# Keeping the residual stream in the output and adding the down parts there by accumulating transfers, with four instead of three of eight gate and up quads by seven products

## The chip, the cores and the metric

The kernel runs on one core of a Trainium2 chip. The metric is the device time of one execution in microseconds (us), as a median of runs. TensorE (PE) multiplies, VectorE (DVE) and ScalarE (ACT) work on what stands in the on-chip memories, GpSimd (POOL) does a little arithmetic and issues a few transfers, SyncE (SP) issues nearly all transfers. Weights come from HBM. They are too large to stay on the chip, so each is read once, while the multiplications run.

## The reference

One layer on an input of 256 rows and 2048 columns, all in float32. The first half mixes tokens with two attentions and two gates and ends in the projection `w_o`, which is added to the input. The second half, which the change touches, is this:

```python
    x = x + (g[:, :, 0] * y_a + g[:, :, 1] * y_b) @ w_o

    gt, up = jnp.split(rms_norm(x, g_ffn) @ w_gate_up, 2, axis=-1)
    return x + (jax.nn.silu(gt) * up) @ w_down
```

`w_gate_up` is 2048 by 2 x 5632, `w_down` is 5632 by 2048.

## The kernel before, in words

**Precision.** Every float32 operand is split into a high and a low part (`h`, `l`) of the type fp32r, and one product of matrices is three matmuls with 512 columns: high by high, high by low, low by high (`mm3`, L427, L428, L429). The high part is a cast on ACT (L220), the low part a subtraction on DVE (L221 for weights, `wl`; it needs the cast).

**Stages.** First the input projection, the attentions, the gates and `w_o` in groups of 512 output columns (PSUM tile `g`). Then the feed-forward half: the 11 column blocks of 512 of the hidden layer are cut into five `PARTS`, one of three blocks and four of two. A part runs its gate and up groups, one per block, and then adds its share of the down projection, in four groups of 512 output columns.

**Quads.** A gate and up group has eight quads, q0 to q7. A quad takes 256 rows of `w_gate_up` and both halves, gate and up: two blocks of rows (256 tokens are two tiles of 128) by two blocks of columns, each with two steps of 128 rows, which is eight products or 24 matmuls. Quads in `FAST`, here q2, q4 and q6, form the same by Winograd's form of Strassen's method with seven products, 21 matmuls. It needs sums of the weight blocks (L844 to L847: four additions of 128x512 on DVE), a split of the raw blocks besides (`rh`, `rl` of 128x1024 and `r` of 128x512), and seven sums of the activations, made once per quad by `job_h` (`hs`, `hsh`, `hsl`). The split of the sums (`wh`, `wl`, 128x2048) is what a plain quad also has. `split_fast` of a fast quad is called before `split` of the quad ahead of it.

**PSUM.** The gate and up groups use all eight banks, held in four tiles: `mA` (products 1 and 6), `mB` (7, 5), `sC` (3, 2), `sD` (4, 0). Fast quads write all but bank 0, plain quads only `sC` and `sD`. After the last fast quad `evac_fast` takes `mA` and `mB` (L663 to L667), after q7 `evac_pair` takes `sC` and `sD` (L677 to L680), applies silu and the product, and a job transposes the result for the down projection. The next group's q0 can write `sC` and `sD` only after that.

**Residual.** `x1[0]` to `x1[3]`, 128x1024 each, hold the residual stream in SBUF from `evac_wo` to the end. Each part's `evac_down` adds a PSUM tile into one of them on DVE (L703), the last part stores the sum.

**Order and buffers.** Up to the last two `w_o` groups the program's order is the code's. From there a list scheduler orders each engine's queue by its own estimates, so the same code can come out in another order. Weight tiles `x` (one quad or four down steps, 1 MB as two transfers of 512 KB) have 3 buffers, so the load of one waits for the `wl` of the third before it. `wh` and `wl` share 6 buffers of 8 KB, enough for three quads, so the cast of a quad waits until PE is done with the third before it. Everything else, `x1`, `rh`, `rl`, `r`, the activations' splits, the group results, comes from 28 buffers of 4 KB (`t4`).

Of the kernel before, what the change touches and what calls it, by code (L numbers as in the profile page):

```python
# [15 lines left out]
ALU = mybir.AluOpType  # L16
# [3 lines left out]
P = 128  # L20
S = 256
NT = S // P
# [17 lines left out]
PARTS = ((0, 3), (3, 5), (5, 7), (7, 9), (9, 11))  # L40
PRIO = 200
NPAIR = KD // 2
FAST = (2, 4, 6)


class Job:
    def __init__(self, gen, after=()):
        self.gen, self.after, self.ready, self.done = gen, tuple(after), 0, False
# [25 lines left out]
class Quad:  # L74


    def __init__(self, group, i):
        self.group, self.i, self.fast = group, i, i in FAST
        plain = [k for k in range(NPAIR) if k not in FAST]
        self.first, self.last = i == plain[0], i == plain[-1]  # L80
        self.first_fast, self.last_fast = i == FAST[0], i == FAST[-1]

# [13 lines left out]
def layer_kernel(ctx: ExitStack, tc: tile.TileContext, a: dict, out: bass.AP):  # L96
    nc = tc.nc
# [11 lines left out]
    def t4(shape, name, dt=F32):  # L109
        return tp.tile(shape, dt, name=name, tag="t4")  # L110

    def small(shape, name):
        return cp.tile(shape, F32, name=name)
# [30 lines left out]
    od = out[0].rearrange("(t p) d -> p t d", p=P)  # L144
# [44 lines left out]
    def gain(name, k):  # L189
        if name == "g_mix":  # L190
            return gmix[:, k:k + 1]
        i = gat[name] + k
        return gcol[:, i:i + 1]

    def rstd_of(ss, d, name):
        n = math.prod(ss.shape[1:])
        v = small(list(ss.shape), name + "_v")
        r = small(list(ss.shape), name)
        nc.gpsimd.tensor_scalar(v, ss, 1.0 / d, EPS, op0=ALU.mult, op1=ALU.add)
        flat = (lambda z: z) if len(ss.shape) == 2 else (lambda z: z.rearrange("p a b -> p (a b)"))  # L200
        nc.gpsimd.tensor_tensor(flat(r), flat(v), mhalf[:, :n], op=ALU.pow)
        return r
# [401 lines left out]
    x1, hP, hjobs, xres = {}, {}, {}, {}  # L604
    ss2 = small([P, NT, 4], "ss2")

    def load_xres(j):
        xres[j] = t4([P, NT, 512], f"xres{j}")
        nc.sync.dma_start(xres[j], xd[:, :, j * 512:(j + 1) * 512])
# [3 lines left out]
    def job_h(i):  # L613

        ps = half_side(f"tr_h{i}").rearrange("p (k s) -> p k s", s=S)
        for k in range(2):
            f = 2 * i + k
            for t in range(NT):
                nc.tensor.transpose(ps[:, k, t * P:(t + 1) * P], x1[f // 4][:, t, (f % 4) * P:(f % 4 + 1) * P], ident)
        g = [gain("g_ffn", 2 * i + k) for k in range(2)]  # L620
        if i not in FAST:
            hP[i] = t4([P, 2, 2, S], f"hP{i}", F32R)
            split_evac(*((hP[i][:, 0, k], hP[i][:, 1, k], ps[:, k], g[k]) for k in range(2)))
        else:
            v, l, h = t4([P, 8, P], f"hs{i}"), t4([P, 7, P], f"hsl{i}", F32R), t4([P, 7, P], f"hsh{i}", F32R)
            nc.scalar.activation(v[:, 0:8:7], ps[:, 0].rearrange("p (t s) -> p t s", t=NT), AF.Copy, scale=g[0])
            nc.scalar.activation(v[:, 1:3], ps[:, 1].rearrange("p (t s) -> p t s", t=NT), AF.Copy, scale=g[1])
            nc.vector.tensor_sub(v[:, 3], v[:, 7], v[:, 2])
            nc.vector.tensor_sub(v[:, 4], v[:, 7], v[:, 0])
            nc.vector.tensor_sub(v[:, 5], v[:, 0], v[:, 3])  # L630
            nc.vector.tensor_sub(v[:, 6], v[:, 1], v[:, 5])
            split_pair(h, l, v[:, :7])
            hq[i] = (h, l)
        return
        yield

    def evac_wo(j):
        def evac(ps, step):
            x1[j] = t4([P, NT, 512], f"x1_{j}")
            nc.vector.tensor_add(x1[j], ps, xres[j])  # L640
            sq = t4([P, NT, 512], f"sq1_{j}")
            for t in range(NT):
                nc.scalar.activation(sq[:, t], x1[j][:, t], AF.Square, accum_out=ss2[:, t, j:j + 1])

            for i in (2 * j, 2 * j + 1):
                hjobs[i] = Job(job_h(i))
                hjobs[i].ready = step + 2
                jobs.append(hjobs[i])
            if j == 3:
                s = small([P, NT], "ss2s")  # L650
                nc.vector.tensor_reduce(s, ss2, axis=AX.X, op=ALU.add)
                st["2"] = rstd_of(s, DM, "r2")
        return evac
# [16 lines left out]
    def evac_pair(half, i, last):  # L670

        def evac(zu, step):
            q = held["q"]
            z, u = zu
            add, sub = nc.vector.tensor_add, nc.vector.tensor_sub
            with tc.high_priority(offset=PRIO):
                add(z[:, 1], q[0], z[:, 1])  # L677
                add(z[:, 0], q[3], z[:, 0])
                add(u[:, 0], q[2], u[:, 0])  # L679
                sub(u[:, 1], q[4], u[:, 1])  # L680
            r = st["2"]
            for t in range(NT):
                nc.scalar.activation(z[:, t], z[:, t], AF.Silu, scale=r[:, t:t + 1])
            for t in range(NT):
                nc.vector.scalar_tensor_tensor(z[:, t], u[:, t], r[:, t:t + 1], z[:, t], op0=ALU.mult, op1=ALU.mult)

            def job():
                ps = held["D" if last else "A"].rearrange("p t (k s) -> p (t k) s", s=S)
                for k in range(4):
                    for t in range(NT):  # L690
                        nc.tensor.transpose(ps[:, k, t * P:(t + 1) * P], z[:, t, k * P:(k + 1) * P], ident)
                h, l = hidT[half].tiles(i)
                split_evac((h, l, ps, None))
                return
                yield
            djobs[half, i] = Job(job())
            djobs[half, i].ready = step + 2
            jobs.append(djobs[half, i])
        return evac

    def evac_down(half, j):
        def evac(ps, step):
            nc.vector.tensor_add(x1[j], ps, x1[j])  # L703
            if half == len(PARTS) - 1:
                nc.sync.dma_start(od[:, :, j * 512:(j + 1) * 512], x1[j])
        return evac

    def evac_last(ps, t):
        for c in range(t + 1):
            w = 512 // (t + 1)  # L710
            s = slice(w * c, w * (c + 1))
            nc.vector.tensor_add(x1[3][:, t, s], ps[:, s], x1[3][:, t, s])
            (nc.scalar if c else nc.sync).dma_start(od[:, t, 1536 + w * c:1536 + w * (c + 1)], x1[3][:, t, s])
# [41 lines left out]
    for half, (j0, j1) in enumerate(PARTS):  # L755
        js = range(j0, j1)
        hidT[half] = Act(f"hid{half}", 4 * len(js))
        for i, j in enumerate(js):
            needs = {k: (lambda k=k: [hjobs[k]]) for k in range(NPAIR)}
            needs[FAST[0]] = lambda: list(hjobs.values())  # L760
            if i:
                needs[FAST[0]] = lambda half=half, i=i: [djobs[half, i - 1]]
            groups.append(Group(W["w_gate_up"], 512 * j, 1024, range(NPAIR), None, evac_pair(half, i, i == len(js) - 1), needs))
        for j in range(4):
            wd = W["w_down"][js[0] * 512:(js[-1] + 1) * 512]
            groups.append(Group(wd, 512 * j, 512, range(4 * len(js)), hidT[half], evac_down(half, j),
                                {k: (lambda k=k, half=half: [djobs[half, k // 4]]) for k in range(4 * len(js))}))
# [161 lines left out]
    def gidx(fn_name, nth=0):  # L929
        return [i for i, n in enumerate(names) if f".{fn_name}." in n][nth]  # L930

    def at(gi, fn, ahead=8):
        early.setdefault(max(0, first_step[gi] - ahead), []).append(fn)
# [9 lines left out]
    for j in range(4):  # L943
        at(gidx("evac_g0", j), lambda j=j: load_bias(j))
        at(gidx("evac_g1", j), lambda j=j: load_bias(4 + j))
        at(gidx("evac_wo", j), lambda j=j: load_xres(j))

    after_evac = {}
    after_evac[gidx("evac_b", 0)] = lambda: jobs.append(prep["kr"])
    after_evac[gidx("evac_b", 6)] = lambda: limited.extend(attn["dil", p] for p in range(4))  # L950
# [28 lines left out]
    for i, (c, ks, first, last) in enumerate(steps):  # L979
# [18 lines left out]
        ps = products(i)  # L998
# [61 lines left out]
```

## Time and profile before

| | |
|---|---|
| median of 3 runs | 1356.28 us (1355.2 to 1356.44) |
| the profiled execution | 1356.11 us, span 1354.3 us |
| around the span | 1.8 us |
| PE busy | 1339.5 us (99%) |
| PE weight loads | 1126.0 us (83%) |
| DVE busy | 949.1 us (70%) |
| ACT busy | 652.2 us (48%) |
| POOL busy | 34.3 us (3%) |
| from HBM, to HBM | 253.97 MB, 2.10 MB |

Durations overlap: matmuls are pipelined, so an engine's pace is read from the starts of neighbouring instructions, not from how long one is shown. A group row gives the count, the busy time, the mean of one in ns, and after the second bar the idle time of the engine just before these, with what ended it. The feed-forward half begins at about 634 us; each part's stretch is its gate and up groups and then the down chunks.

### The profile page before, as it was taken

To read this page: it belongs to the slowest core of one execution; us is meant where nothing else is said; L and a number is where in the kernel's file an instruction comes from. 1 tells how busy PE (TensorE), PEld (TensorE's weight loads), DVE (VectorE), ACT (ScalarE), POOL (GpSimd) and SP (SyncE) were. 2 spreads that over 40 slices of the span, in tenths; PEclk is the share of its full clock that TensorE was granted. 3 is DMA by queue.
4 is the path that set the end of the run, shared out by engine and by line. 5 is a ranking of instruction groups with operands and counts; after the bars stand their busy time and mean duration, and the time that the engine had idled before them with its cause. 6 is when DMAs were issued, how large, how long until landed. Compare 5 with 4: busy or idle time off the path is not lost.

```text
span 1354.3 us, 16169 instructions
## 1 busy us (share of the span) xinstructions
PE 1339.5 (99%) x6243; PEld 1126.0 (83%) x6243; DVE 949.1 (70%) x949; ACT 652.2 (48%) x724; POOL 34.3 (3%) x41
## 2 busy tenths in 40 slices
PE   8999999999999999999999999999999999999998
PEld 6899999988888888888788888888878888888886
DVE  5566777677645655567789756886798579857973
ACT  6455555454444444455455434454445345534541
POOL 1011112000000000000000000000000000000000
PEclk9999999999999999999999999999999999999999
DMA  7555555656556766676546665565457654754662
GB/s 247 179 175 161 161 170 167 184 161 176 174 186 205 212 188 202 209 235 207 201 158 213 221 187 183 191 213 190 157 185 245 191 186 172 229 190 163 214 214 93
DMA packets 138205, 257.14 MB, mean 190 GB/s; under 512 B 9192, under 2 KB 28688, under 8 KB 138128
## 3 DMA queue, kind: packets, MB, share of 16 engines
q1 hardware_dynamic: 137760, 255.96, 58.9%
q8 instruction: 49, 0.80, 0.2%
q14 instruction: 28, 0.23, 0.1%
q10 hardware_dynamic: 144, 0.13, 0.0%
q0 software_dynamic: 224, 0.01, 0.0%
HBM read 253.97 MB, written 2.10 MB: 189 GB/s over the span
## 4 chain that ended last, share of the span: by engine, by line
PE 94%; DVE 2%; issue 1%; DMA 1%; ACT 1%; SPq 0%; DVEq 0%; ACTq 0%
PE g L429 14%; PE g L427 14%; PE g L428 13%; PE sC L427 6%; PE sC L429 6%; PE sC L428 6%; PE mA L427 4%; PE mA L429 4%; PE mA L428 4%; PE sD L429 4%; PE sD L427 4%; PE sD L428 4%; PE mB L428 3%; PE mB L429 3%; PE mB L427 3%
## 5 line engine op out<-in xcount | busy, mean ns | idle before, releaser
L220 ACT CAST wh<-x 128x1024 fp32r<-128x1024 f32 (+3 forms) x349 | 465.3, 1352 | 437.0 <-DVE x L847 127.7
L221 DVE TENSOR_TENSOR wl<-x,wh 128x2048 fp32r<-128x2048 f32 x132 | 300.8, 2289 | 134.5 <-ACT wh L220 132.7
L221 DVE TENSOR_TENSOR wh<-x,wh 128x1024 fp32r<-128x1024 f32 (+2 forms) x217 | 250.6, 1172 | 113.1 <-ACT wh L220 111.9
L427 PE MATMUL g<-wh,xTh 128*128 128x512 f32 (+1 forms) x544 | 210.6, 387 | 0.6 <-ACT xTh L212 0.6
L429 PE MATMUL g<-wh,xTl 128*128 128x512 f32 (+1 forms) x544 | 207.9, 382 | 0.6 <-DVE xTl L217 0.6
L428 PE MATMUL g<-wh,xTh 128*128 128x512 f32 (+1 forms) x544 | 207.9, 382 | 0.0
L429 PEld LDWEIGHTS g<-wh,xTl 128*128 128x128 f32 x544 | 102.8, 189 | 17.6 <-DVE xTl L217 1.4
L427 PEld LDWEIGHTS g<-wh,xTh 128*128 128x128 f32 x544 | 102.8, 189 | 15.9 <-ACT xTh L212 0.9
L428 PEld LDWEIGHTS g<-wh,xTh 128*128 128x128 f32 x544 | 102.9, 189 | 15.4 <-DVE wh L221 0.4
L427 PE MATMUL sC<-wh,hP 128*128 128x512 f32 x220 | 86.1, 391 | 1.6 <-DVE u L679 1.5
L429 PE MATMUL sC<-wh,hP 128*128 128x512 f32 x220 | 85.7, 390 | 0.0
L429 PE MATMUL sD<-wh,hP 128*128 128x512 f32 x220 | 85.7, 389 | 0.0
L428 PE MATMUL sC<-wl,hP 128*128 128x512 f32 x220 | 85.7, 389 | 0.0
L427 PE MATMUL sD<-wh,hP 128*128 128x512 f32 x220 | 85.7, 389 | 0.0
L428 PE MATMUL sD<-wl,hP 128*128 128x512 f32 x220 | 85.7, 389 | 0.0
L220 ACT CAST rh<-x 128x1024 fp32r<-128x1024 f32 x33 | 34.7, 1051 | 36.1 <-DMA x<-in_w_gate_up_dram 36.1
L427 PEld LDWEIGHTS sC<-wh,hP 128*128 128x128 f32 x220 | 41.3, 188 | 12.3 <-issue 4.0
L427 PE MATMUL g<-wh,mTh 128*128 128x512 f32 x128 | 50.5, 394 | 0.0
L429 PE MATMUL g<-wh,mTl 128*128 128x512 f32 x128 | 49.9, 390 | 0.0
L428 PE MATMUL g<-wh,mTh 128*128 128x512 f32 x128 | 49.9, 390 | 0.0
L427 PEld LDWEIGHTS sD<-wh,hP 128*128 128x128 f32 x220 | 41.3, 188 | 8.6
L428 PEld LDWEIGHTS sD<-wl,hP 128*128 128x128 f32 x220 | 41.3, 188 | 8.6
(675 smaller groups left out, 2390.7 us busy)
## 6 DMA issues: line engine op xcount, KB each, us to landing
x<-in_w_gate_up_dram SPq DMA_DIRECT2D x176, 512.0 KB, 4.7
x<-in_w_down_dram SPq DMA_DIRECT2D x88, 512.0 KB, 5.0
x<-in_w_in_dram SPq DMA_DIRECT2D x79, 512.0 KB, 4.2
x<-in_w_in_dram SPq DMA_DIRECT2D x56, 448.0 KB, 3.6
x<-in_w_o_dram SPq DMA_DIRECT2D x32, 512.0 KB, 4.4
x<-in_w_o_mla_dram SPq DMA_DIRECT2D x16, 512.0 KB, 4.9
x<-in_w_o_dil_dram SPq DMA_DIRECT2D x16, 512.0 KB, 4.6
x<-in_w_ukv_dram SPq DMA_DIRECT2D x8, 512.0 KB, 4.0
```

Of the source, the lines that this page charges most:

```text
L220: nc.scalar.copy(h, x)
L221: nc.vector.tensor_sub(l, x, f32(h))
L427: nc.tensor.matmul(ps, ah, bh, start=first, stop=False)
L428: nc.tensor.matmul(ps, ah, bl, start=False, stop=False)
L429: nc.tensor.matmul(ps, al, bh, start=False, stop=last)
```

## The change

`FAST` gets q5 as a fourth quad, next to q4 and q6. The residual stream no longer stays in SBUF. After `w_o`, each `x1[j]` is stored to the output. A down part but the last is copied from PSUM to SBUF on ACT (`y`) and added to the output by a transfer that accumulates in memory, issued from POOL. Ahead of the last part's down groups the four tiles are loaded back on the SP queue (`load_x1`), and the end is as before.

```diff
-FAST = (2, 4, 6)
+FAST = (2, 4, 5, 6)
@@ evac_wo
+            nc.sync.dma_start(od[:, :, j * 512:(j + 1) * 512], x1[j])
             for i in (2 * j, 2 * j + 1):
@@ evac_down
-            nc.vector.tensor_add(x1[j], ps, x1[j])
-            if half == len(PARTS) - 1:
-                nc.sync.dma_start(od[:, :, j * 512:(j + 1) * 512], x1[j])
+            cols = od[:, :, j * 512:(j + 1) * 512]
+            if half < len(PARTS) - 1:
+                y = t4([P, NT, 512], f"y{half}_{j}")
+                nc.scalar.copy(y, ps)
+                nc.gpsimd.dma_start(cols, y, accum_op=ALU.add)
+            else:
+                nc.vector.tensor_add(x1[j], ps, x1[j])
+                nc.sync.dma_start(cols, x1[j])
         return evac
+
+    def load_x1(j):
+        x1[j] = t4([P, NT, 512], f"x1b_{j}")
+        nc.sync.dma_start(x1[j], od[:, :, j * 512:(j + 1) * 512])
@@ hooks by step
+    for j in range(4):
+        at(gidx("evac_down", 4 * (len(PARTS) - 1) + j), lambda j=j: load_x1(j), 2)
```

The lines below the insertions move down by up to ten: L844 to L847 become L854 to L857, L664 to L667 become L665 to L668, and L677 to L680 become L678 to L681.

DVE's queue in the second gate and up group of the second part. The tiles are numbered by quad: 265 is q4, 266 is q5, 267 is q6, 268 is q7. Before:

```order
L221 TENSOR_TENSOR wl265_6782<-x265_6700,wh265_6781 128x2048
L221 TENSOR_TENSOR wl266_6821<-x266_6742,wh266_6820 128x2048
L221 TENSOR_TENSOR rl267_6810<-x267_6785,rh267_6809 128x1024
L221 TENSOR_TENSOR r267_6811<-x267_6785,r267_6811 128x512
L844 TENSOR_TENSOR x267_6785<-x267_6785 128x512
L845 TENSOR_TENSOR x267_6785<-x267_6785 128x512
L846 TENSOR_TENSOR x267_6785<-x267_6785 128x512
L847 TENSOR_TENSOR x267_6785<-x267_6785 128x512
L221 TENSOR_TENSOR wl267_6852<-x267_6785,wh267_6851 128x2048
L221 TENSOR_TENSOR wl268_6880<-x268_6824,wh268_6879 128x2048
```

After, from the row behind `wl265`:

```order
L221 TENSOR_TENSOR rl266_6832<-x266_6792,rh266_6831 128x1024
L221 TENSOR_TENSOR r266_6833<-x266_6792,r266_6833 128x512
L854 TENSOR_TENSOR x266_6792<-x266_6792 128x512
L855 TENSOR_TENSOR x266_6792<-x266_6792 128x512
L221 TENSOR_TENSOR rl267_6871<-x267_6846,rh267_6870 128x1024
L856 TENSOR_TENSOR x266_6792<-x266_6792 128x512
L221 TENSOR_TENSOR r267_6872<-x267_6846,r267_6872 128x512
L857 TENSOR_TENSOR x266_6792<-x266_6792 128x512
L854 TENSOR_TENSOR x267_6846<-x267_6846 128x512
L855 TENSOR_TENSOR x267_6846<-x267_6846 128x512
L856 TENSOR_TENSOR x267_6846<-x267_6846 128x512
L221 TENSOR_TENSOR wl266_6882<-x266_6792,wh266_6881 128x2048
```

Between `wl` of q4 and `wl` of q5 there was nothing, and now stand eleven instructions; the last sum of q6 and then `wl` of q6 and q7 follow.

PE's queue at the start of q5 in the same group. Before, a plain quad:

```order
L427 MATMUL sD_5118<-wh266_6820,hP5_4990 128x512
L428 MATMUL sD_5118<-wl266_6821,hP5_4990 128x512
L429 MATMUL sD_5118<-wh266_6820,hP5_4990 128x512
L427 MATMUL sD_5118<-wh266_6820,hP5_4990 128x512
L428 MATMUL sD_5118<-wl266_6821,hP5_4990 128x512
```

After:

```order
L427 MATMUL mA_5125<-r266_6833,hsh5_4995 128x512
L428 MATMUL mA_5125<-r266_6833,hsh5_4995 128x512
L429 MATMUL mA_5125<-r266_6833,hsl5_4994 128x512
L427 MATMUL mA_5125<-wh266_6881,hsh5_4995 128x512
L427 MATMUL mB_5126<-wh266_6881,hsh5_4995 128x512
L427 MATMUL sC_5127<-rh266_6831,hsh5_4995 128x512
L428 MATMUL sC_5127<-rl266_6832,hsh5_4995 128x512
L429 MATMUL sC_5127<-rh266_6831,hsl5_4994 128x512
L428 MATMUL mA_5125<-wl266_6882,hsh5_4995 128x512
```

The first matmul that reads `wl` of q5 was the second of the quad and is now the ninth. In the first group of such a part it is the fifth (the three on `r`, one on `wh`, then `wl`), and in the three groups of the first part the nineteenth, because products of q6 on `rh` are drawn ahead of it.

DVE's queue at the end of the first part's first group, where `wl225` and `wl226` belong to the next group's q0 and q1 and the rows on `sC` and `sD` release these tiles for them. Before:

```order
L221 TENSOR_TENSOR wl226_5385<-x226_5311,wh226_5384 128x2048
L678 TENSOR_TENSOR z0_5366<-sC_5117,z0_5366 128x512
L679 TENSOR_TENSOR u0_5367<-sC_5117,u0_5367 128x512
L677 TENSOR_TENSOR z0_5366<-sD_5118,z0_5366 128x512
L680 TENSOR_TENSOR u0_5367<-sD_5118,u0_5367 128x512
```

After:

```order
L221 TENSOR_TENSOR wl225_5357<-x225_5304,wh225_5356 128x2048
L679 TENSOR_TENSOR z0_5384<-sC_5127,z0_5384 128x512
L680 TENSOR_TENSOR u0_5385<-sC_5127,u0_5385 128x512
L221 TENSOR_TENSOR wl226_5403<-x226_5332,wh226_5402 128x2048
L678 TENSOR_TENSOR z0_5384<-sD_5128,z0_5384 128x512
L681 TENSOR_TENSOR u0_5385<-sD_5128,u0_5385 128x512
```

The split of the next q1 has moved from ahead of all four rows to between the two pairs; PE's queue follows with the products into `sC` first.

## The prediction

> **What bounds the kernel now.** I read the page's busy times first, then busy time by stretch, then PE's and DVE's rows around one q5.
>
> ```profile
> PE 1339.5 (99%) x6243; PEld 1126.0 (83%) x6243; DVE 949.1 (70%) x949; ACT 652.2 (48%) x724; POOL 34.3 (3%) x41
> ```
>
> PE is busy nearly all the time, so a matmul less is worth its pitch, unless PE then waits. DVE's 70% is a mean over stages. The feed-forward stretches, with busy time and count for each engine:
>
> ```profile
> core 0: us, PE busy (x) PEld busy (x) DVE busy (x) ACT busy (x) POOL busy (x), PEclk, DMA share, GB/s
> 679.00:722.00 43.00, 42.84 (x192) 35.09 (x192) 38.55 (x38) 23.67 (x20) 0.00 (x0) 1.00 0.57 196
> 764.00:830.00 66.00, 66.00 (x297) 54.76 (x296) 37.15 (x25) 26.56 (x17) 0.00 (x0) 1.00 0.61 193
> 830.00:872.00 42.00, 42.00 (x186) 34.58 (x185) 34.22 (x32) 19.86 (x15) 0.00 (x0) 1.00 0.59 201
> 872.00:915.00 43.00, 42.84 (x193) 35.31 (x193) 37.23 (x36) 21.20 (x17) 0.00 (x0) 1.00 0.59 195
> ```
>
> The first is a gate and up group of part 0, the second a part's down chunks, the last two the first and second group of part 1. In the down chunks DVE is idle 29 of 66 us. In the groups it is idle only 4.5, 7.8 and 5.8 us: that is what the change has to live on. The clock is full, and the DMA engines have room.
>
> **PE's gain.** Three rows give the pitch: the start of q4, q5 and q6 in part 1's second group.
>
> ```profile
> 894.52 0.39 PE L427 MATMUL mA<-r,hsh 128*128 128x512 f32 x1
> 899.28 0.39 PE L427 MATMUL sD<-wh,hP 128*128 128x512 f32 x1
> 904.72 0.39 PE L427 MATMUL mA<-r,hsh 128*128 128x512 f32 x1
> ```
>
> A fast quad of 21 takes 899.28 - 894.52 = 4.76 us, a plain one of 24 takes 5.44: 0.2267 us each. Making q5 fast saves 0.68 us a group, in 11 groups 7.5 us if nothing waits.
>
> The Trainium skill, "TensorE: Matmul & The Clock Gate", section "Back-to-back issue gap", puts the sustained spacing at 512 columns at about 131 ns; by it the gain would be estimated at 33 x 0.131 = 4.3 us, and the sum below would come out 3.2 us higher. This trace disagrees, at 227 ns, and the measurement decides.
>
> **What DVE gets.** Its rows in that same group, and ACT's casts that release them:
>
> ```profile
> 888.89 2.28 DVE L221 TENSOR_TENSOR wl<-x,wh 128x2048 fp32r<-128x2048 f32 x1
> 892.63 2.29 DVE L221 TENSOR_TENSOR wl<-x,wh 128x2048 fp32r<-128x2048 f32 x1 [1.46 <-ACT wh L220]
> 895.05 1.23 DVE L221 TENSOR_TENSOR rl<-x,rh 128x1024 fp32r<-128x1024 f32 x1
> 896.20 0.68 DVE L221 TENSOR_TENSOR r<-x,r 128x512 fp32r<-128x512 f32 x1
> 896.91 0.69 DVE L844 TENSOR_TENSOR x<-x 128x512 f32<-128x512 f32 x1
> 899.09 0.69 DVE L847 TENSOR_TENSOR x<-x 128x512 f32<-128x512 f32 x1
> 901.84 4.49 DVE L221 TENSOR_TENSOR wl<-x,wh 128x2048 fp32r<-128x2048 f32 x2 [2.05 <-ACT wh L220]
> 890.69 1.91 ACT L220 CAST wh<-x 128x2048 fp32r<-128x2048 f32 x1 [3.04 <-PE mA L428]
> 893.97 1.05 ACT L220 CAST rh<-x 128x1024 fp32r<-128x1024 f32 x1 [1.37 <-DMA x<-in_w_gate_up_dram]
> 894.93 0.61 ACT L220 CAST r<-x 128x512 fp32r<-128x512 f32 x1
> ```
>
> `wl` of q4, `wl` of q5, then q6's `rl`, `r`, four sums, `wl` of q6 and of q7. By pitch `rl` takes 1.15, `r` 0.71, a sum (899.09 - 896.91)/3 = 0.73, `wl` 2.2. A fast q5 adds 1.15 + 0.71 + 4 x 0.73 = 4.8 us to DVE, 1.6 us to ACT (1.05 + 0.61). DVE's 38.55, 34.22 and 37.23 become 43.3, 39.0 and 42.0, against 42.3 of PE (a shortened group). So in two of three kinds of group DVE has as much to do as PE, and the order decides. ACT stays at half.
>
> **Second group of a part (1 to 4), walked.** DVE's order after has eleven instructions between `wl` of q4 and `wl` of q5. `wl` of q4 ends at 891.1. q5's tile has landed by 890.69, when ACT casts it; its `rh`, cast there instead, ends about 891.8. Then: `rl5` 892.9, `r5` 893.6, two sums 895.1, `rl6` 896.2 (its `rh` ends 895.02, no wait), a sum 896.95, `r6` 897.65, q5's last sum 898.4, three sums of q6 900.55. ACT's cast of q5's sums starts at 898.4 and ends 900.3. `wl5` runs 900.55 to 902.75. PE's q5 starts at 899.28, and its ninth matmul, the first to read `wl5`, is due at 899.28 + 8 x 0.2267 = 901.1: a stall of 1.65 us. Next late is `wl6`: last sum 903.45, cast 905.35, `wl6` until 907.6, against a need at 902.75 + 13 x 0.2267 + 8 x 0.2267 = 907.5: 0.1. `wl7` follows at 909.8, in time. Group: 1.65 + 0.1 - 0.68 = **+1.1**.
>
> **First group of a part (1 to 4), walked.**
>
> ```profile
> 844.16 0.69 DVE L847 TENSOR_TENSOR x<-x 128x512 f32<-128x512 f32 x1
> 856.36 0.39 PE L427 MATMUL sD<-wh,hP 128*128 128x512 f32 x1
> 868.69 2.28 DVE L221 TENSOR_TENSOR wl<-x,wh 128x2048 fp32r<-128x2048 f32 x1
> 872.31 0.47 PE L427 MATMUL sC<-wh,hP 128*128 128x512 f32 x1 [0.16 <-DVE u L679]
> ```
>
> 844.16 is q4's last sum, 856.36 q5's start on PE, 868.69 the split of the next group's q1, 872.31 PE's start of that group, right behind the release of `sC`. From 844.85 the order after holds `rl5`, `r5`, a sum, `wl4`, a sum, `rl6`, a sum, `r6`, a sum, three sums, `wl5`: 2 x 1.15 + 2 x 0.71 + 7 x 0.73 + 2 x 2.2 = 13.2, until 858.05. PE reads `wl5` in the fifth matmul, 856.36 + 0.91 = 857.3: stall 0.75. At the end the next q1's tile decides. Its buffer comes free with `wl6` (about 862.8), the load takes about 5, the cast 1.9: `wl` starts about 870.0 instead of 868.69, ends 872.2, and with one row on `sC` behind it PE restarts at 872.95 instead of 872.31. That is **+0.64** with the 0.68 already in it. DVE then stands 1.3 later and PE only 0.64, so the next group's q2, whose splits come straight after, stalls about **+0.6**.
>
> Per part 0.64 + 0.6 + 1.1 = 2.35; four parts: **+9.4**.
>
> **Part 0.** Its groups in the profile:
>
> ```profile
> 695.39 2.28 DVE L221 TENSOR_TENSOR wl<-x,wh 128x2048 fp32r<-128x2048 f32 x1
> 715.38 0.68 DVE L664 TENSOR_TENSOR z<-mA,u 128x512 f32<-128x512 f32 x1
> 721.61 0.69 DVE L677 TENSOR_TENSOR z<-sD,z 128x512 f32<-128x512 f32 x1
> ```
>
> These are `wl` of q4, the start of `evac_fast`, and the first row on `sD`; the pair on `sC` ends there, and PE restarts. In the order after, each group end is one `wl` behind: the next q0's split comes after `evac_fast`, q1's between the pairs. `sC` is still free at 715.38 + 2.7 + 2.2 + 1.3 = 721.6, but `sD` one `wl` and a pair later, 725.2; PE's queue has sixteen products into `sC` first, 16 x 0.2267 = 3.6 us, which just covers it. DVE then starts the next group 2.4 us later than before, and its queue has no gap up to q4. From 695.39, with `rl`, `r` of two quads and eight sums behind it, q5's `wl` would end about 709.8 without that delay, 712.2 with it. PE reaches q5 at 721.6 - 69 x 0.2267 = 706.0, and needs this `wl` only as nineteenth, 710.1: stall 2.1, less 0.68: **+1.5** for the second and third group, 3.0. The first group, where no evacuation precedes, I put at 0.
>
> **The part's end.**
>
> ```profile
> 921.60 0.98 PE L691 MATMUL sD<-ident,z 128*128 128x128 f32 x7 [0.96 <-DVE z L685]
> PE sD L691 <- DVE z L685: 1.7, 2, 1.0
> ```
>
> Before, transposes at part ends wait 1.7 us in two places for the product, behind a `wl` in DVE's queue. After, both products stand ahead of that `wl`: **-1.7**.
>
> **The residual.**
>
> ```profile
> L703 DVE TENSOR_TENSOR x<-mA,x 128x1024 f32<-128x1024 f32 x9 | 11.0, 1221 | 7.0 <-PE mA L429 7.0
> L210 ACT CAST mTh<-tr_mT 128x1024 fp32r<-128x1024 f32 x4 | 4.1, 1015 | 14.2 <-PE tr_mT L244 14.2
> out_dram<-x SPq DMA_DIRECT2D x3, 512.0 KB, 2.8
> x<-in_w_gate_up_dram SPq DMA_DIRECT2D x176, 512.0 KB, 4.7
> L221 DVE TENSOR_TENSOR hsl<-hs,hsh 128x896 fp32r<-128x896 f32 x3 | 3.3, 1092 | 3.2 <-ACT hsh L220 3.2
> ```
>
> DVE loses 16 additions of 1.22 us, ACT gets 16 copies; nearest is ACT's cast out of PSUM, 1.02 us. Both lie in the down chunks, where DVE has 29 and ACT 39 us idle; a tile freed 0.2 us sooner or 1 us later moves nothing, since the chunks rotate over four tiles: 0. The 16 accumulating transfers have no row here. Their ends: 2.8 us (a store) and 2.8 + 4.7 = 7.5 (read and write in turn); nearer the upper, as the target is read too. Either is short against a down group of 16.5 us (66/4), on POOL's queue, where nothing else waits: 0. The next part's accumulation waits for the last one's, 100 us earlier. The four stores after `w_o` stand on SP's queue ahead of weight loads and wait for the residual sums; each sum is done before SP comes to that load, at 2.8 us a store: 0, at most 4 x 2.8. The four reloads precede down loads of the last part: 4 x 4.7 us at 0.6 DMA share, 0 to 5 us if the last loads come late. The sums of activations for q5 add 4 small additions and a split of 1.1 us on DVE before part 0, where the first fast quad is ready ahead: 0 to 1.
>
> The Trainium skill, "DMA: Bandwidth & Descriptors", section "Anatomy of one DMA — SWDGE (gpsimd) path", fits 2.0 us plus bytes over 436 GB/s for a transfer issued by POOL: an estimate of 3.2 us for 512 KB. No run here shows an accumulating one; by it the sum stays as it is.
>
> **Sum.** 1356.1 + 9.4 + 3.0 - 1.7 = 1366.8, against the profiled 1356.11; the median of runs is 0.2 higher: **1367**.
>
> **Rivals.**
> - *Stalls stay hidden, faster.* For it: DVE has 5.8 to 7.8 us idle in the groups of parts 1 to 4, more than 4.8, and four of its instructions per part leave. If all is covered: 1356.1 - 7.5 - 1.7 = 1346.9; with half of the PE gain, 1351. The place is `wl5` behind eleven instructions; the point is a mean stall of 0.68 + 1.7/11 = 0.84 us a group. If ACT casts q5's `rh` a microsecond sooner, or q5's tile lands sooner, the second group's stall falls from 1.65 to that. Against: in part 0 only 4.5 us are idle.
> - *Accumulating transfers collide with weight loads.* Those of a part's last chunks run while the next part's first tiles load. A late tile delays DVE's chain by 2.8 (a store) to 4.7 us (a load), at four part starts: +11 to +19, 1378 to 1386. Against: the DMA engines are 40% free, and x tiles wait for casts there.
> - *DVE simply as bound:* each group as long as DVE's work, 43.3 against PE's 43.0 before in part 0, less than before elsewhere: about 1352 to 1357. It is what the two groups would reach with a perfect order; the walked order isn't that.
>
> **Chances.** The walk 0.60 (own range 1358 to 1376: half of its stalls to one and a half), hidden 0.22, DVE as bound 0.06, collision 0.12. What a measurement can tell from no change is 0.2%, 2.7 us: 1353.6 to 1359.0. Of the hidden and bound cases 0.20 lie below, 0.08 within; of the walk 0.03 within. Faster 0.20, same 0.11, slower 0.69. The range cuts off the fully hidden end and the worst collision, about 0.1 each: 1350 to 1383.
>
> **What would show it.** Right: in the waits, PE waiting for DVE's `wl` of q5, 1 to 2 us in most groups; PE's busy sum about 7 us lower; DVE busy about 30 us higher (52 of q5, less 20); no transposes waiting 1 us at part ends. Wrong: PE waits for `wl` of q5 under 0.7 us in most groups (then faster), or PE waits at q2 to q4 of parts 1 to 4 for DMA-late tiles (then the collision), or a gap in the last part's down chunks from the reloads.

## The result and the profile after

The changed kernel takes 1378.91 us (median of 5 runs, 1375.34 to 1379.76) against 1356.44 us of the kernel before on the same chip: ratio 1.0155, interval 1.0136 to 1.0175, 22.5 us slower. The profiled execution has a span of 1377.0 us, 22.7 more than before. From the page of the changed kernel, the busy times:

```profile
PE 1342.9 (98%) x6210; PEld 1122.7 (82%) x6210; DVE 977.5 (71%) x1002; ACT 686.1 (50%) x763; POOL 53.3 (4%) x57
```

33 matmuls are gone (6243 to 6210), DVE has 28 us more and ACT 34. PE's busy time is 3.4 us more in spite of the matmuls that left. The clock accounts for 5.8 us of that, below; the waits add to it too, because the last matmul before a wait is shown in its full length. By stretch, with the same columns as before: second and third group of part 0, first and second group of part 1.

```profile
681.10:727.10 46.00, 43.45 (x188) 34.09 (x189) 42.61 (x44) 25.26 (x22) 0.00 (x0) 1.00 0.54 183
727.10:773.00 45.90, 43.36 (x188) 34.34 (x189) 42.41 (x43) 23.59 (x21) 0.00 (x0) 1.00 0.54 183
839.20:885.40 46.20, 42.90 (x182) 34.71 (x180) 39.04 (x39) 23.78 (x20) 1.18 (x1) 0.96 0.70 209
885.40:927.90 42.50, 42.17 (x188) 34.62 (x189) 39.29 (x40) 21.73 (x18) 0.00 (x0) 1.00 0.51 175
```

DVE's busy times are those foreseen in the first two kinds of group (43.3, 39.0) and 2.7 us less in the third (42.0), but the lengths are not. All stretches, from one group's first matmul to the next's, in us:

| | before | after | difference |
|---|---|---|---|
| up to the feed-forward half | 634.7 | 637.4 | +2.7 |
| part 0: three groups | 44.1, 42.9, 42.6 | 43.7, 46.1, 45.9 | -0.4, +3.1, +3.3 |
| parts 1 to 4: first group | 41.8, 42.5, 41.8, 41.8 | 46.2, 45.2, 45.1, 46.2 | +4.4, +2.7, +3.3, +4.4 |
| parts 1 to 4: second group | 42.6, 42.5, 42.6, 42.7 | 42.5, 43.4, 43.5, 42.3 | -0.1, +0.9, +0.8, -0.4 |
| down chunks of all parts, and the end | 251.7 | 249.6 | -2.1 |

Of the first line, 1.6 us stand at 80 us already, far ahead of any changed instruction. Two thirds of the loss is in the first group of parts 1 to 4. What PE waits for, from the list of waits (total in us, times, longest):

```profile
PE mA L428 <- DVE wl L221: 8.9, 8, 1.8
PE sC L427 <- DVE u L680: 6.9, 4, 2.0
PE mB L428 <- DVE wl L221: 1.3, 2, 0.7
PE sD L428 <- DVE wl L221: 0.9, 2, 0.5
PE sD L692 <- DVE z L686: 0.2, 1, 0.2
```

The splits were foreseen. Of the first row, four waits of 1.7 to 1.8 us stand at `wl` of q5 in the first groups of parts 1 to 4, the other four are 0.2 to 0.7. The second row was not foreseen: at the end of four groups PE waits for the rows that release `sC`. DVE's rows there, end of part 1's first group:

```profile
882.64 0.68 DVE L679 TENSOR_TENSOR z<-sC,z 128x512 f32<-128x512 f32 x1
883.96 0.69 DVE L678 TENSOR_TENSOR z<-sD,z 128x512 f32<-128x512 f32 x1 [0.64 <-PE sD L429]
884.57 0.68 DVE L680 TENSOR_TENSOR u<-sC,u 128x512 f32<-128x512 f32 x1
885.16 0.68 DVE L681 TENSOR_TENSOR u<-sD,u 128x512 f32<-128x512 f32 x1
```

A row on `sD` has moved between the two on `sC`. It waits for PE's last product, and the release of `sC` waits behind it.

**Transfers.** The accumulating transfers (median us to landing), then the DMA share around the last two of part 0: after, and the same stretch before.

```profile
out_dram<-y POOLq DMA_DIRECT2D x16, 512.0 KB, 6.5
836.00:849.00 13.00, 13.00 (x59) 10.74 (x59) 10.01 (x9) 7.71 (x7) 2.37 (x2) 1.00 0.92 205
827.30:840.30 13.00, 13.00 (x59) 10.74 (x59) 10.88 (x11) 5.19 (x4) 0.00 (x0) 1.00 0.38 124
```

They are issued at 836.9 and 840.7 us and meet the tile of part 1's q4. Its two loads, issued at 838.0 and 838.6, and below them the loads of the same stretch before (those of 830.0 to 838.8):

```profile
DMA to landing us min/median/max: 6.8/7.2/7.6
DMA to landing us min/median/max: 4.1/4.5/5.0
```

**Clock.** Behind the stall at `wl` of q5, PE's rows and the granted clock:

```profile
867.96 0.50 PE L428 MATMUL mA<-wl,hsh 128*128 128x512 f32 x1 [1.82 <-DVE wl L221]
869.33 0.63 PE L427 MATMUL mB<-wh,hsh 128*128 128x512 f32 x1
869.76 0.63 PE L428 MATMUL mB<-wl,hsh 128*128 128x512 f32 x1
868.80:872.30 3.50, 3.50 (x10) 2.71 (x9) 1.75 (x1) 3.50 (x2) 0.00 (x0) 0.54 0.84 273
```

The pitch is 0.43 instead of 0.227 us for some 3 us, at a granted clock of 0.54. Parts 1 to 4 have one such stretch each: in parts 1 and 4 behind the wait at q5 of the first group, in parts 2 and 3 behind the wait on `sC`, at the start of the second group. The matmuls' excess over 0.2267 us there adds up to 5.8 us, half of it in first and half in second groups, and it makes the +0.9 and +0.8 of the table.

### The profile page after: what moved, and what is told of

Its sections match the earlier page's. It is cut to its first block, busy times and chain, and to the rows that moved or that the text cites. A ratio compares the mean times of both kernels' runs of the same rounds, so it can differ in the third digit from the quotient of the medians.

```text
span 1377.0 us, 16268 instructions
## 1 busy us (share of the span) xinstructions
PE 1342.9 (98%) x6210; PEld 1122.7 (82%) x6210; DVE 977.5 (71%) x1002; ACT 686.1 (50%) x763; POOL 53.3 (4%) x57
## 4 chain that ended last, share of the span: by engine, by line
PE 75%; DVE 10%; DMA 6%; issue 4%; ACT 3%; SPq 1%; DVEq 0%; ACTq 0%
PE g L429 13%; PE g L427 13%; PE g L428 13%; DMA x<-in_w_gate_up_dram 4%; DVE wl L221 4%; PE sC L427 4%; PE sC L428 4%; PE sC L429 4%; PE mA L428 4%; PE mA L429 3%; PE mA L427 3%; ACT wh L220 3%; PE mB L429 2%; PE mB L428 2%; PE mB L427 2%
## 5 line engine op out<-in xcount | busy, mean ns | idle before, releaser
L220 ACT CAST rh<-x 128x1024 fp32r<-128x1024 f32 x44 | 46.3, 1052 | 61.8 <-DMA x<-in_w_gate_up_dram 61.7
L427 PE MATMUL sC<-wh,hP 128*128 128x512 f32 x176 | 69.9, 397 | 7.1 <-DVE u L680 6.9
L428 PE MATMUL sD<-wl,hP 128*128 128x512 f32 x176 | 69.2, 393 | 0.9 <-DVE wl L221 0.9
L429 PE MATMUL sD<-wh,hP 128*128 128x512 f32 x176 | 69.4, 394 | 0.0
L428 PE MATMUL sC<-wl,hP 128*128 128x512 f32 x176 | 69.2, 393 | 0.0
L429 PE MATMUL sC<-wh,hP 128*128 128x512 f32 x176 | 69.1, 392 | 0.0
L427 PE MATMUL sD<-wh,hP 128*128 128x512 f32 x176 | 69.0, 392 | 0.0
L221 DVE TENSOR_TENSOR rl<-x,rh 128x1024 fp32r<-128x1024 f32 x44 | 53.6, 1219 | 4.4 <-ACT rh L220 4.4
L427 PEld LDWEIGHTS sC<-wh,hP 128*128 128x128 f32 x176 | 33.6, 191 | 16.3 <-ACT z L684 6.6
L708 POOL DMA_DIRECT2D out_dram<-y x16 | 19.1, 1197 | 578.2 <-ACT y L707 578.2
```

What stands on the lines that cost most here:

```text
L220: nc.scalar.copy(h, x)
L221: nc.vector.tensor_sub(l, x, f32(h))
L427: nc.tensor.matmul(ps, ah, bh, start=first, stop=False)
L428: nc.tensor.matmul(ps, ah, bl, start=False, stop=False)
L429: nc.tensor.matmul(ps, al, bh, start=False, stop=last)
L708: nc.gpsimd.dma_start(cols, y, accum_op=ALU.add)
```

## The experiments

My theory behind the forecast: DVE's 4.8 us for a fast q5, in the order it has. The rivals: the accumulating transfers, and the residual part as a whole. Times are set against the kernel before in the same batch.

**The residual part alone.**

```diff
-FAST = (2, 4, 5, 6)
+FAST = (2, 4, 6)
```

> The residual part alone: the residual stream in the output and the accumulating transfers as in the changed kernel, but three fast quads (q2, q4, q6) as before. If the loss is DVE's work for the fourth fast quad, this stands at the time before, 1353 to 1358. If the accumulating transfers, which delay the first tiles of the next part by about 3 us, are the loss, each of four parts loses 2 to 3 us here too: 1362 to 1368. If both are needed together (late tiles on a full DVE), this is within 3 us of before.

1371.65 us against 1358.40, ratio 1.0102 (1.0079 to 1.0124): 13.3 us slower, without a fast q5. DVE's work for q5 can't be the whole loss. The first groups of parts 1 and 2, and the longest wait:

```profile
837.00:879.80 42.80, 41.70 (x185) 34.19 (x183) 34.33 (x32) 21.19 (x16) 1.18 (x1) 1.00 0.70 220
968.10:1013.10 45.00, 42.17 (x185) 34.05 (x183) 34.33 (x32) 21.17 (x16) 1.18 (x1) 1.00 0.67 210
PE mA L619 <- ACT hs L627: 4.1, 1, 4.1
```

DVE's work is that of before (34.2), and yet they are 1.0 and 2.4 us longer. The wait of 4.1 us stands in part 0's first group, once.

**The same without the accumulating transfers.**

```diff
-                nc.gpsimd.dma_start(cols, y, accum_op=ALU.add)
```

> Three fast quads as before, the residual stored to the output and loaded back, but no accumulating transfers (the first four parts' down shares are left out of the result); the order of PE, DVE and ACT is that of the run with three fast quads. If the accumulating transfers' collision makes the 9 us that the groups of parts 1 to 4 lost there, and the first part's 5 us come from the stores after w_o: 1361 to 1365. If the collision is small: 1368 to 1372.

1362.44 us against 1357.86, ratio 1.0033 (1.0019 to 1.0048): 8.7 us of the 13.3 are gone. The order on PE, DVE and ACT is the same row by row, so this is the transfers alone. The same two groups:

```profile
836.40:878.20 41.80, 41.64 (x185) 34.20 (x183) 34.08 (x32) 21.20 (x16) 0.00 (x0) 1.00 0.58 202
965.30:1007.10 41.80, 41.65 (x184) 34.18 (x183) 34.08 (x32) 21.17 (x16) 0.00 (x0) 1.00 0.57 201
```

41.8 each, as part 1's was before. DMA share falls from 0.70 to 0.58.

**The stores after `w_o` from POOL's queue besides.**

```diff
-            nc.sync.dma_start(od[:, :, j * 512:(j + 1) * 512], x1[j])
+            nc.gpsimd.dma_start(od[:, :, j * 512:(j + 1) * 512], x1[j])
```

> As the run before it, and the four stores of the residual after w_o issued from POOL's queue instead of SP's. If these stores, each waiting for its residual sum, hold back the weight tiles behind them on SP, and this makes the 4 us stall in the first group: the time of before, 1354 to 1359. If the stall is the order's: as the run before it.

1359.92 us, ratio 1.0015 (1.0005 to 1.0024). In the profile the feed-forward half begins 2.0 us sooner than in the run before, at 635.0, though the two spans are about the same (1358.4 and 1357.9), since part 0's first group takes 49.2 instead of 47.6 us. In the run before, the first two stores had waited on SP for the residual sum, and with them the `xres` loads (the input rows for the next sum) behind them, issued at 568.9 and 597.4 instead of 563.4 and 592.7. But the long wait stays (3.8 us), so SP's queue is not its cause. Nor is the order: through part 0's groups the rows of PE, DVE and ACT stand as in the kernel before. The tile whose `rh` starts that chain arrives 3.2 us late (this run, then the kernel before):

```profile
629.78 1.05 ACT L220 CAST rh<-x 128x1024 fp32r<-128x1024 f32 x1 [2.60 <-DMA x<-in_w_gate_up_dram]
626.56 1.05 ACT L220 CAST rh<-x 128x1024 fp32r<-128x1024 f32 x1 [2.08 <-DMA x<-in_w_gate_up_dram]
```

A store of 512 KB is issued at 615.4, 0.9 us ahead of six loads of the first tiles, which land 6.8 to 8.5 us after their issue instead of 4.3 to 6.1. That the store makes them late is likely, but no run took it away. With four fast quads the same lateness costs nothing: in the run with all three costs taken away, below, the six land at the same times within 0.3 us, and PE's longest wait in this group is 0.6 us.

**The changed kernel without its accumulating transfers.** The edit is that of the second experiment.

> The changed kernel without its 16 accumulating transfers: the down parts of the first four parts are copied to SBUF and not added (this part of the result is left out). If DVE's work and order alone make the loss: unchanged, 1375 to 1380. If the transfers' collision with the first tiles of a part is what makes the first group's stall 2 us instead of 0.75, and with it the lower clock behind it: 3 us less in each of four parts, 1365 to 1368.

1371.61 us against 1358.40, ratio 1.0101 (1.0080 to 1.0123): 13.2 us slower instead of 22.5, with the same order on PE, DVE and ACT. About 9 us of the loss are the transfers. The waits:

```profile
PE sC L427 <- DVE u L680: 8.8, 4, 2.7
PE mA L428 <- DVE wl L221: 3.2, 8, 0.8
```

The wait for `wl` on `mA` falls from 8.9 to 3.2 us, that for `u` grows from 6.9 to 8.8. At `wl` of q5 in the first groups of parts 1 to 4 PE now waits 0.2 to 0.8 us instead of 1.7 to 1.8, so the late tile made these waits longer, and the end of the group costs without the transfers too. So 13 us have another cause.

**q5 without its sums, then without splits and sums.**

```diff
+        raws[c] = {1: (r[:, 0], r[:, 1]), 3: (rh[:, 0], rl[:, 0]), 2: (rh[:, 1], rl[:, 1])}
+        if chunks[c][3].i == 5:
+            return
         add(x[:, 1], x[:, 0], x[:, 1])
```

> The changed kernel with q5's split rl, rh, r kept and only its four sums left out, 2.9 us of DVE in each group. If DVE's load is the loss, in proportion: 1360 to 1366 (a stall of about 1.5 us less in each of 11 groups). If the tile's late arrival is the loss, the sums matter little: 1374 to 1379.

1364.23 us, ratio 1.0043 (1.0027 to 1.0060): 5.8 us slower instead of 22.5. 2.9 us of DVE's work a group, 32 us in all, were worth about 17. The wait for `wl` on `mA` falls to 2.7 us; that for `u` on `sC` does not fall (9.9).

```diff
-        if q and q.fast and c not in raws:
+        if q and q.fast and q.i != 5 and c not in raws:
...
+            raw = raws.pop(c) if q.i != 5 else {1: (h[:, 1], l[:, 1]), 3: (h[:, 2], l[:, 2]), 2: (h[:, 3], l[:, 3])}
...
```

> The changed kernel with q5's seven products on PE, but with operands taken from a plain split of its blocks: its rl, r and four sums on DVE and rh, r on ACT are left out (so q5's products are of the unsummed blocks). If DVE's 4.8 us per group are the loss, PE's 33 matmuls less are now seen: 1345 to 1350. If the accumulating transfers are the loss: 1356 to 1362.

1357.05 us, ratio 0.9994 (0.9978 to 1.0011), with runs from 1352.94 to 1361.38. The time lies where the transfers' theory had it: with q5's work on DVE gone, what is left against PE's gain is about their share. In the profile, of the slowest of these runs, PE still waits 8.6 us for `u` on `sC`; in the next run, without the transfers and the stores on SP, 1.7. With the run before it this says that both are at work. In both runs the order shifts too, which they don't separate.

**All three costs taken away.** The last run but without accumulating transfers and with the stores on POOL's queue.

> Four fast quads on PE with all three suspected costs taken away: q5 without its own splits and sums (operands from a plain split), no accumulating transfers, the stores after w_o on POOL's queue. If these are the causes, PE's 33 matmuls (7.5 us) are now seen whole: 1346 to 1350. If something else takes them: 1353 or more.

1351.82 us against 1357.86, ratio 0.9954 (0.9939 to 0.9969): 6.0 us faster, of 7.5 expected. The groups of part 1:

```profile
830.60:871.70 41.10, 40.96 (x181) 33.61 (x180) 34.06 (x32) 21.17 (x16) 0.00 (x0) 1.00 0.58 204
871.70:913.80 42.10, 42.08 (x188) 34.65 (x189) 37.77 (x36) 20.89 (x17) 0.00 (x0) 1.00 0.57 198
```

41.1 against 41.8: the 0.68 us of PE, whole; in the second group 42.1 against 42.6. DVE has 34.1 and 37.8, near the 34.0 and 36.9 of the kernel before. The steps between the runs add up to the loss, as they must: -6.0 with nothing against it; +19.2 from there to the changed kernel without transfers (q5's work on DVE and ACT with its order, and the stores on SP, which cost 2.5 in the runs with three quads); +9.3 for the transfers; together 22.5.

**`sC` first.**

```diff
+            with tc.high_priority(offset=2 * PRIO):
+                add(z[:, 0], q[3], z[:, 0])
+                add(u[:, 0], q[2], u[:, 0])
             with tc.high_priority(offset=PRIO):
                 add(z[:, 1], q[0], z[:, 1])
-                add(z[:, 0], q[3], z[:, 0])
-                add(u[:, 0], q[2], u[:, 0])
                 sub(u[:, 1], q[4], u[:, 1])
```

> The changed kernel with one rule for DVE's order at a group's end: the two rows on sC before the two on sD (in the changed kernel the first groups of parts 1 to 4 have z of sC, z of sD, u of sC, u of sD; ACT's order stays). If these four places cost PE 6.9 us of waits, as the trace of the changed kernel has them, sC is released 1.3 us sooner in each and no lower clock follows: 5 to 8 us off, 1370 to 1374. If the wait is only late DVE work, whatever comes first: 1377 to 1380.

1377.15 us, ratio 1.0127 (1.0100 to 1.0154), not told apart from the changed kernel's. In the profile, the wait on `sC` falls, and the stretches at the low clock go (0.4 us of excess pitch instead of 5.8):

```profile
PE mA L428 <- DVE wl L221: 8.9, 11, 1.8
PE sC L427 <- DVE u L679: 4.3, 3, 1.6
PE mB L428 <- DVE wl L221: 2.2, 3, 0.9
```

With 1.4 us behind ACT's `z` the wait on `sC` is 5.7 us in all, from 6.9. The first groups of parts 1 to 4 are 4.5 us shorter together, but DVE's work is not less, and part 4's second group loses 1.6 us that it had not lost. The time expected, 1370 to 1374, was missed: the two rows come first, yet PE still waits 1.3 to 1.6 us at each of the four places.

**The last two down groups in sequence.**

```diff
-                    if two + 2 == len(groups):
+                    if two == gi + 2:
                         continue
...
-            if two + 2 == len(groups):
+            if two == gi + 2:
                 for e in (two, two + 1):
```

> The changed kernel with the last two down groups of each part one after the other instead of interleaved, so that the accumulating transfer of the third is issued some 5 us sooner and only that of the fourth meets the next part's first tiles. If the collision costs 7 us: 2 to 5 us less, 1374 to 1377. If it is only DVE's order: 1378 to 1380.

1375.03 us, ratio 1.0116 (1.0082 to 1.0149): as expected, but the four runs lie between 1371.58 and 1379.06 and the intervals overlap, so it is not settled. In the profile, of the fastest of them, the first groups of parts 2 and 3 are 1.8 and 3.3 us shorter than in the changed kernel, that of part 1 is 1.6 longer.

**`rl` and `r`'s low part on POOL.**

```diff
-        split_pair(rh, rl, x[:, 2:4])
-        split_pair(r[:, 0], r[:, 1], x[:, 1])
+        nc.scalar.copy(rh, x[:, 2:4])
+        nc.gpsimd.tensor_sub(rl, x[:, 2:4], f32(rh))
+        nc.scalar.copy(r[:, 0], x[:, 1])
+        nc.gpsimd.tensor_sub(r[:, 1], x[:, 1], f32(r[:, 0]))
```

> The changed kernel with rl and r's low part of every fast quad subtracted on POOL instead of DVE, which takes about 7.5 us a group off DVE. If DVE's load is the loss and POOL does 128x1024 in 2 to 3 us beside DVE: 1355 to 1365. If POOL is slower than about 5 us for it, or slows DVE: 1375 or more.

1467.69 us, ratio 1.0795 (1.0770 to 1.0820). POOL's rows, and two of DVE's four sums beside them:

```profile
L852 POOL TENSOR_TENSOR rl<-x,rh 128x1024 fp32r<-128x1024 f32 x44 | 122.6, 2787 | 653.2 <-ACT rh L851 653.2
L854 POOL TENSOR_TENSOR r<-x,r 128x512 fp32r<-128x512 f32 x44 | 84.4, 1918 | 15.5 <-ACT r L853 15.5
L856 DVE TENSOR_TENSOR x<-x 128x512 f32<-128x512 f32 x44 | 54.2, 1231 | 70.2 <-POOL r L854 70.2
L857 DVE TENSOR_TENSOR x<-x 128x512 f32<-128x512 f32 x44 | 36.8, 843 | 0.9
```

POOL takes 2.8 and 1.9 us where DVE took 1.2 and 0.7, DVE's sums take 1.23 and 0.84 instead of 0.69 us, and 70 us of DVE's idle time end with POOL's `r`, which the sums must wait for. The mean granted clock falls to 0.971 (0.994 in the changed kernel): some 36 us of the loss are matmuls at a longer pitch behind the waits. All three edits together were worse still:

> All three together: sC first at a group's end, the last two down groups in sequence, rl and r's low part on POOL. If these are the three causes, the gain of 33 matmuls is left with little against it: 1346 to 1354, below both kernels. If POOL slows DVE or the order shifts the waits elsewhere: 1360 or more.

1486.53 us, ratio 1.0939 (1.0909 to 1.0969).

**What can be mended without POOL's arithmetic:** `sC` first, the down groups in sequence, the stores on POOL's queue.

> The full computation of the changed kernel, with sC first at a group's end, the last two down groups in sequence and the stores after w_o on POOL's queue. Each takes part of one cause away, DVE's work for q5 stays: 1364 to 1370, still above the kernel before. If DVE's work is dearer than the rest: 1372 or more; if cheaper: under 1362.

1371.80 us, ratio 1.0103 (1.0087 to 1.0120): 7 us better than the changed kernel, still 14 us behind the kernel before. No version with the whole computation beat the kernel before.

## Why the prediction was right or wrong

The sign and the range held (1378.9 in 1350 to 1383), but the sum gave +10.7 and the time moved by 22.5. The walk's own range, 1358 to 1376, was missed; the stated one held because it reached up for the collision, which had a chance of 0.12. That is luck in part. Its steps:

- **PE's gain: right.** 0.68 us a group is what the first groups show in the run with all costs taken away, and 6.0 of 7.5 us arrive in its time.
- **DVE's load: right.** 43.3, 39.0 and 42.0 us foreseen, 42.6, 39.0 and 39.3 measured, in all 28 us for about 30. That a full DVE with a fixed order makes PE wait is what the runs without q5's sums and splits show.
- **Part 0: mis-sized.** +1.5 for each of two groups, +3.1 and +3.3 measured. The working is loose, too: the rows up to q5's `wl` add up to 709.4, not 709.8, and 2.1 less 0.68 is 1.4. I let DVE's 2.4 us of delay reach PE at q5 only. PE pays it at q2 and q3 first, then again at q5:

```profile
696.19 0.50 PE L428 MATMUL mB<-wl,hsh 128*128 128x512 f32 x1 [0.67 <-DVE wl L221]
699.00 0.50 PE L428 MATMUL sD<-wl,hP 128*128 128x512 f32 x1 [0.47 <-DVE wl L221]
715.83 0.51 PE L428 MATMUL mA<-wl,hsh 128*128 128x512 f32 x1 [0.67 <-DVE wl L221]
```

  These are 1.8 us; two waits for ACT's casts add 0.6, and by the starts of the rows each of the five costs PE some 0.3 us more than is shown, which makes the 3.8 us (3.1 and the 0.68 of PE's gain).

- **First group of parts 1 to 4: the largest miss.** +0.64 foreseen, +4.4, +2.7, +3.3 and +4.4 measured. The walk started from q4's tile in time; its loads took 2.7 us longer (7.2 against 4.5), so `wl` of q5 stalled PE 1.7 to 1.8 us, not 0.75; without the transfers it stalled 0.2 to 0.8. At the group's end I took the order of the rows on `sC` and `sD` from before, and PE waited 1.5 to 2.0 us there. It was in the new order, and I had looked at it in part 0 only. And a stall was priced at its length: the low clock behind four of these eight cost 5.8 us more, half of it here and half in the second groups of parts 2 and 3.
- **Second group: too dear.** +1.1 and +0.6 foreseen, -0.4 to +0.9 measured, and without the low clock all four would be shorter than before. PE waits for `wl` of q5 there 0.3 us at most, not 1.65. That PE's loss in the first group gave DVE the time back is likely, but not tested.
- **The part's end: right.** The wait for the product fell from 1.7 to 0.2 us; the down stretches are 2.1 us shorter.
- **The residual at 0: wrong.** It alone costs 13.3 us: 8.7 by the accumulating transfers, 2.5 by the stores on SP, 2 that the runs don't attribute (in that trace part 0's first group, behind the late tile above, is 5.1 us longer than before). The reloads are free, as forecast: the last part's down chunks take 49.7 us before and after. I compared one transfer with a down group's 16.5 us and found it short. Its price lies in what runs beside it: the loads of the next part's first tiles. That was the second rival, with a chance of 0.12 and four times 2.8 to 4.7 us; the runs show 9. What I had held against it, free DMA engines, was a mean over the stretch, 0.6; where it matters the share is 0.92. The bound for the transfer itself (2.8 to 7.5, nearer the upper) was right: 6.5 us. The Trainium skill, "DMA: Bandwidth & Descriptors", section "Anatomy of one DMA — SWDGE (gpsimd) path", has a fit that gives an estimate of 3.2 us; this trace disagrees for an accumulating one. The shortest plain store from POOL's queue, in the run that has such stores, took 3.2.
- **The stores on SP: wrong.** I asked whether a sum is done before SP comes to the next weight load, and left out the `xres` load that stands between.
- **The signs: in part misleading.** A wait of 1 to 2 us at `wl` of q5 stood in four of 11 groups; in the other seven it was 0.7 or less, which I had named as the sign of a faster kernel. PE's busy sum rose by 3.4 us instead of falling by 7. The collision did not show as waits at q2 to q4, but at q5, behind DVE.

So the forecast was right in direction for half of the reasons: DVE's part was there, and the part put at nothing was as large.

## What to carry to other kernels

A transfer that is off the path is priced by what it slows, in the microseconds in which it runs: look at the DMA share of that stretch, not of the stage, and at which loads are under way. When work moves in a kernel whose second engine is nearly full, follow the delay to its first consumer and check the new order at every place that is repeated, since it may differ between parts. A gain of 0.5% on the bound engine is gone with one extra wait of 0.7 us a group.

## What the runs showed of the hardware that I had not expected

- A wait of 1.8 us in PE was followed by a granted clock of 0.54 over some 3 us, at a pitch of 0.43 us; other waits of about that length (at 1001 us, `wl` of q5 in part 2) had none behind them. The Trainium skill, "TensorE: Matmul & The Clock Gate", section "Part 1: The HAM clock gate", puts the cold pitch for 512 columns at 426.7 ns, which this trace shows, and gives about 3.4 us of idle time as the step to it, more than PE idled here.
- An accumulating transfer of 512 KB lands after 6.5 us (6.1 to 8.5). Plain stores of that size from SP took 2.7 to 5.6 us in the same trace (median 2.8 of three at the end, 4.4 of four after `w_o`). The loads of a tile beside two accumulating transfers took 7.2 us instead of 4.5.
- POOL's subtractions slow DVE's sums, from 0.69 to between 0.84 and 1.23 us each. The Trainium skill, "SBUF — State Buffer", section "SBUF: two separate sides", has DVE and GpSimd share a pair of ports that one instruction holds as a whole; the trace agrees with that in its direction.
